# MLP second product of a decoder block: seven half products in Strassen's form for eight, on a hi/lo-split fp32 matmul

## The chip, the cores and the metric

The kernel runs on one core of one Trainium2 chip. The metric is the device time of one execution in microseconds (us), as the median of several runs. Engines: PE is TensorE (matmul), PEld its weight loads, DVE VectorE, ACT ScalarE, POOL GpSimd, SP SyncE, which here only issues DMAs.

## The reference

One inference step of a one-layer decoder, for 2048 prompt tokens and 64 sample tokens (8 sequences of 8). A mixer (forgetting attention and a matrix memory) gives `mix`; the part in question comes after it:

```python
x1  = layer_norm(ALPHA * x + mix @ w_o)          # (2112, 1024)
hid = square(relu(x1 @ w1))                      # (2112, 4096)
y   = layer_norm(ALPHA * x1 + hid @ w2)          # (2112, 1024)
```

All is fp32. The sample tokens also attend to a paged cache of 8192 past positions per sequence; that attention (the functions below it called "sample attention") is independent of the prompt tokens until its result enters `mix` of the 64 sample tokens.

## The kernel before, in words

The program is traced in phases: projections (A), prompt attention (B), output projection and first layer norm (O), MLP (C). Sample attention runs beside them in small steps: `tick(us)` adds up an amount for each piece of main work and, each time 5 us (`PACE_C`) have come together in phase C, lets one step of a generator run. A step's PE work is sQ (scores, with cached keys gathered by GpSimd into `kT`), sT (transposes) and sO (values, gathered by GpSimd into `vt`, or into `xr` while `vx["more"]` lends a second landing place). A scheduler then orders each engine's instructions once and for all by its own estimate of their times; on the chip each engine works through its list in that order and waits on semaphores.

A product in fp32 is made of three matmuls: `split_hi` (ACT, a copy into the type fp32r) and `split_lo` (DVE, the difference to it) turn an operand into hi and lo, and `mm3` (L152 to L155) adds hi·hi, hi·lo and lo·hi in PSUM. `piece` (L1058) loads 128x1024 of a weight into a `wr` buffer and splits it into `wh`, `wl`.

Phase C goes over four blocks `CB` of tokens: four tiles of 128 (W = 512), the last with the 64 sample tokens as tile 16 too (W = 576). x1 of a block lies transposed in SBUF as `x1h`, `x1l`. For each of 16 columns blocks `fc` of 256 of w1:

- `hidden(fc)`: two halves f of 128 hidden columns, each 8 x 3 matmuls into a `ph` PSUM tile (two pieces of 288 tokens where W = 576), then Relu and Square on ACT into `hq`, then its split into `hh`, `hl`.
- `output(fcs)`: two weight pieces of w2 per fc; for each token tile and each half of the 1024 columns, 2 x 3 matmuls of 128x512 into a `py` tile, and one DVE instruction (L1292, at fc 0 L1290) that adds the `py` tile to the row `y` of that token tile in SBUF.

`output` runs one fc behind `hidden`; the last two are done together, tile by tile, each tile followed at once by `layer_norm` and its store. Before that last output `load` brings in and transposes x1 of the next block (L1097). At fc 14 `vx["more"]` is taken away, at fc 13 of the third block sample attention must have ended; `sampled()` (L1215) then does the output projection and first layer norm of the 64 sample tokens, through DRAM (`dmix`, `dx1`), so that they can enter the fourth block as tile 16.

Buffers: `wr` 4, `wh` 5, `wl` 4, `hh` and `hl` 4, one `hq`, `ph` 3 and `py` 3 PSUM tiles.

```python
def mm3(ps, wh, wl, xh, xl, first, stop):
    T.matmul(ps, wh, xh, start=first, stop=False)
    T.matmul(ps, wh, xl, start=False, stop=False)
    last["PE"] = T.matmul(ps, wl, xh, start=False, stop=stop)
```

Of the kernel before, what the change touches and what calls it, by code (L numbers as in the profile page):

```python
# [52 lines left out]
def body(ctx, tc, I, O, stages):  # L53
# [95 lines left out]
        if eng is None:  # L149
            last["DVE"] = r  # L150

    def mm3(ps, wh, wl, xh, xl, first, stop):  # L152
        T.matmul(ps, wh, xh, start=first, stop=False)  # L153
        T.matmul(ps, wh, xl, start=False, stop=False)  # L154
        last["PE"] = T.matmul(ps, wl, xh, start=False, stop=stop)  # L155

    def layer_norm(x, np_, g, b, wk, tg, eng=None):
        st = wk.tile([128, 2, 6], F32, name="ln_st")
# [886 lines left out]

    def raw():

        return pcw.tile([128, 1024], F32, name="wr", bufs=4)

    def landing(n=128):  # L1050

# [12 lines left out]
    def piece(src, wr=None):  # L1064

        if wr is None:
            wr = raw().rearrange("p (k c) -> p k c", k=src.shape[1])
            SY.dma_start(wr, src)
        k = wr.shape[1]
        wh = C["pc"].tile([128, 1024], F32R, name="wh", bufs=5).rearrange("p (k c) -> p k c", k=k)  # L1070
# [31 lines left out]
    def phase_o(halves):  # L1102
# [19 lines left out]
        def weights(hf):  # L1122
            for q in range(4):
                r = halves.pop(0) if halves else half_wo(hf, q)
                if hf == 0:
                    h, l = piece(None, r)
                    if q == 0:
                        V.memset(pc.tile([128, 512], F32, name="hq", bufs=1)[:, 0:1], 0.0)
# [31 lines left out]
        unit(0, 0)  # L1160
        weights(1)
        unit(1, 0)
        gb = [bcast(I[f"ln1_{x}"], 0, D, f"{x}1", pcw, tag="wr", bufs=4) for x in "gb"]
        unit(0, 1)
        m[2] = mix(2, G)
        end(0)
# [37 lines left out]
    def phase_c():  # L1204
        es = ExitStack()
        pc, ph = C["pc"], es.enter_context(tc.tile_pool(name="ph", bufs=1, reuse_waits="tile"))
        ppc = es.enter_context(tc.tile_pool(name="ppc", bufs=1, space=PSUM, reuse_waits="tile"))
        w2, wo = I["w2"][0], I["w_o"][0]

        def vecs(l):  # L1210
            g = bcast(I[f"ln{l}_g"], 0, D, f"g{l}", pcw, tag="wr", bufs=4)
            b = bcast(I[f"ln{l}_b"], 0, D, f"b{l}", pcw, tag="wr", bufs=4)
            return g, b

        def sampled():  # L1215

            mx = pc.tile([128, 8, 64], F32, name="mxs", tag="hq", bufs=1)
            SY.dma_start(mx, dmv[:, :, S:])
            mh = ph.tile([128, 8, 64], F32R, name="mhs", tag="hh", bufs=4)
            ml = ph.tile([128, 8, 64], F32R, name="mls", tag="hl", bufs=4)  # L1220
            split_hi(mh, mx)
            split_lo(ml, mx, mh)
            y = row()
            SY.dma_start(y[:64], x_of(16))
            for c in range(4):
                ps = ppc.tile([128, 512], F32, name="py", bufs=3)[:64, :256]
# [5 lines left out]
                V.scalar_tensor_tensor(y[:64, s], y[:64, s], ALPHA, ps, op0=OP.mult, op1=OP.add)  # L1232
            layer_norm(y[:64], 64, *vecs(1), pc, "1")
            SY.dma_start(dx1[S:], y[:64])

        CB = [[0, 1, 2, 3], [4, 5, 6, 7], [8, 9, 10, 11], [12, 13, 14, 15, 16]]
        def load(ci):
            for i, t in enumerate(CB[ci]):
                x1_turn(t, i, x1_load(t), lambda: ppc.tile([128, 4, 128], F32, name="px2", tag="ph", bufs=3))
            vx["more"] = landing  # L1240

        vx["more"] = landing
        for ci, blk in enumerate(CB):
            W = sum(tok_n(t) for t in blk)
            off = {t: i * 128 for i, t in enumerate(blk)}
            xh, xl = C["x"]
            ys = {}
            pieces = [(0, 512)] if W == 512 else [(0, 288), (288, 576)]
            H = {}

            def hidden(fc):
                w1p = C.pop("w1", None) or w1_pieces(fc)
                H[fc] = []
                for f in range(2):
                    hh = ph.tile([128, 576], F32R, name="hh", bufs=4)
                    hl = ph.tile([128, 576], F32R, name="hl", bufs=4)
                    H[fc].append((hh, hl))
                    for (a, b) in pieces:
                        ps = ppc.tile([128, 512], F32, name="ph", tag="ph", bufs=3)[:, :b - a]
# [3 lines left out]
                        hq = pc.tile([128, 512], F32, name="hq", tag="hq", bufs=1)[:, :b - a]  # L1263
                        A.activation(hq, ps, AF.Relu)
                        A.activation(hq, hq, AF.Square)
                        split_hi(hh[:, a:b], hq)
                        split_lo(hl[:, a:b], hq, hh[:, a:b])
                        tick((b - a) * 0.01)

            def output(fcs):  # L1270
                w2p = [piece(w2[fc * 256 + k * 128:fc * 256 + k * 128 + 128].rearrange("(k p) c -> p k c", p=128)) for fc in fcs for k in range(2)]
                h = [x for fc in fcs for x in H.pop(fc)]
                if 15 in fcs:
                    gb = vecs(2)
                for t in blk:
                    n = tok_n(t)
                    s = slice(off[t], off[t] + n)
                    if 0 in fcs:
                        ys[t] = row()
                        with tc.issue_after(last["ACT"].ins):  # L1280
                            A.dma_start(ys[t][:n], dx1[tok_r(t):tok_r(t) + n])
                    for hf in range(2):
                        cs = slice(hf * 512, (hf + 1) * 512)
# [4 lines left out]
                        y = ys[t][:n, cs]  # L1288
                        if 0 in fcs:
                            V.scalar_tensor_tensor(y, y, ALPHA, ps, op0=OP.mult, op1=OP.add)  # L1290
                        else:
                            V.tensor_tensor(y, y, ps, op=OP.add)  # L1292
                        tick(1.28 * len(fcs))
                    if 15 in fcs:
                        layer_norm(ys[t][:n], n, *gb, pc, "2", V if ci == 3 else G)
                        d = (O["y_sample"].rearrange("b t d -> (b t) d") if t == 16 else O["y_prompt"][0, t * 128:(t + 1) * 128])
                        SY.dma_start(d, ys[t][:n])

            for fc in range(16):
                if fc == 14:  # L1300
                    vx["more"] = None
                hidden(fc)
                if fc == 15 and ci < 3:
                    take_back()
                    load(ci + 1)
                if fc > 0:
                    output([14, 15] if fc == 15 else [fc - 1])
                if fc == 13 and ci == 2:
# [394 lines left out]
def laid_in(a):  # L1703
# [10 lines left out]
    a["state_conv"] = a["state_conv"][0].reshape(NB, 3, 8, 128).transpose(3, 2, 0, 1)  # L1714
    a["state_n"] = a["state_n"][0].transpose(2, 0, 1)
    a["w_o2"] = a["w_o"][0].reshape(4, 2, 128, 2, 512).transpose(3, 0, 2, 1, 4).reshape(2, 4, 128, 1024)
    a["w1"] = a["w1"][0].reshape(2, 4, 128, 16, 256).transpose(3, 0, 2, 1, 4).reshape(16, 2, 128, 1024)
    return {k: np.ascontiguousarray(v) for k, v in a.items()}

# [11 lines left out]

# [9 lines left out]
```

## Time and profile before

| | |
|---|---|
| median of 3 runs | 3387.81 us (3377.21 to 3388.4) |
| profiled execution, its own time | 3392.21 us |
| its span, first to last instruction | 3390.5 us |
| mean granted TensorE clock | 0.985 |
| PE busy | 3263.4 us (96%) |
| DVE busy | 1884.5 us (56%) |
| ACT busy | 1361.9 us (40%) |
| POOL busy | 870.8 us (26%) |
| moved by DMA | 650.48 MB, mean 192 GB/s |

Phase C begins at about 1610 us of the span and lasts to its end. In the rows of the profile, `py` are matmuls of the second product, `ph` of the first; "128*128 128x512" are the rows and columns of the stationary operand and the shape of the result. A group row reads: line, engine, operation, output<-input, shapes, count, then busy us and mean ns of one, then idle time before it and what ended that. A row of the timeline reads: start, duration, engine, line, operation, operands, count. Matmuls overlap in the pipeline: the pace is the distance of their starts, not their duration.

### The profile page before, as it was taken

How to read it: one execution, taken by the hardware profiler on the slowest of the kernel's cores; microseconds unless marked ns; L12 is line 12 of the kernel's file. 1: busy time of each engine (PE TensorE's matmuls, PEld its weight loads, DVE VectorE, ACT ScalarE, POOL GpSimd, SP SyncE). 2: the span in 40 equal slices, each digit the busy share in tenths (PEclk: the TensorE clock that was granted, in tenths of full speed). 3: DMA queues.
4: the chain of work that ended last, by engine and by line, in shares of the span. 5: the costliest groups of instructions: out<-in, count | busy, mean ns of one | idle time of the engine just before them, and what ended most of it. 6: DMA issues, size and time to landing. Idle time of an engine off the chain costs nothing.

```text
span 3390.5 us, 58224 instructions
## 1 busy us (share of the span) xinstructions
PE 3263.4 (96%) x22065; PEld 2642.0 (78%) x22065; DVE 1884.5 (56%) x4774; ACT 1361.9 (40%) x2795; POOL 870.8 (26%) x925
## 2 busy tenths in 40 slices
PE   8999998999889999999999999999999999999998
PEld 8998998888756667676777777777776777888886
DVE  6847474464388887434444455445554445644545
ACT  4333343333278888313332333233333423433332
POOL 0131242323322222475223324323252110100000
PEclk9999999999999999999999999999999999999999
DMA  5575766766662322687777768667588444432221
GB/s 180 156 217 187 223 216 231 244 225 218 204 167 83 92 84 52 238 289 243 283 239 241 246 231 292 249 215 273 208 291 278 171 167 147 162 122 81 87 75 66
DMA packets 316001, 650.48 MB, mean 192 GB/s; under 512 B 61001, under 2 KB 175049, under 8 KB 314825
## 3 DMA queue, kind: packets, MB, share of 16 engines
q1 hardware_dynamic: 239032, 367.55, 35.4%
q0 software_dynamic: 74304, 270.57, 22.1%
q10 hardware_dynamic: 2384, 8.65, 0.7%
q8 instruction: 174, 2.85, 0.4%
q14 instruction: 107, 0.87, 0.1%
HBM read 593.82 MB, written 52.83 MB: 191 GB/s over the span
## 4 chain that ended last, share of the span: by engine, by line
PE 48%; DMA 3%; DVE 2%; issue 1%; ACT 1%; POOL 1%; another core or an unknown queue 0%; SPq 0%; POOLq 0%; ACTq 0%; DVEq 0%
PE py L153 7%; PE py L155 7%; PE py L154 7%; PE ph L153 7%; PE ph L155 7%; PE ph L154 7%; PE sO L1598 3%; PE sQ L1486 2%; DMA wr<-w 2%; PE sT L1555 1%; DVE wl L148 1%; PE pw L154 0%; PE pw L155 0%; PE pw L153 0%
## 5 line engine op out<-in xcount | busy, mean ns | idle before, releaser
L1292 DVE TENSOR_TENSOR y<-y,py 128x512 f32<-128x512 f32 (+1 forms) x476 | 324.1, 685 | 420.9 <-PE py L155 337.0
L145 ACT ACTIVATE wh<-wr 128x1024 fp32r<-128x1024 f32 x268 | 278.0, 1058 | 548.3 <-PE py L155 228.0
L153 PE MATMUL ph<-x1h,wh 128*128 128x512 f32 (+1 forms) x1280 | 458.4, 358 | 4.0 <-ACT wh L145 3.1
L154 PE MATMUL ph<-x1l,wh 128*128 128x512 f32 (+1 forms) x1280 | 456.7, 357 | 0.2 <-issue 0.2
L155 PE MATMUL ph<-x1h,wl 128*128 128x512 f32 (+1 forms) x1280 | 455.5, 357 | 0.9 <-issue 0.8
L153 PE MATMUL py<-wh,hh 128*128 128x512 f32 (+1 forms) x1088 | 438.4, 404 | 8.5 <-DVE y L1290 4.8
L1463 POOL DMA_INDIRECT kT<-cache_k,idxK x256 | 261.6, 1022 | 671.5 <-PE sQ L1486 610.3
L154 PE MATMUL py<-wl,hh 128*128 128x512 f32 (+1 forms) x1088 | 432.2, 397 | 0.6 <-DVE wl L148 0.6
L155 PE MATMUL py<-wh,hl 128*128 128x512 f32 (+1 forms) x1088 | 431.7, 397 | 0.0
L148 DVE TENSOR_TENSOR wl<-wr,wh 128x1024 fp32r<-128x1024 f32 x268 | 338.8, 1269 | 160.0 <-PE ph L155 47.1
L153 PE MATMUL pm<-xh,whi 128*128 128x256 f32 (+1 forms) x1024 | 301.9, 295 | 0.7 <-issue 0.4
L154 PE MATMUL pm<-xl,whi 128*128 128x256 f32 (+1 forms) x1024 | 297.9, 291 | 2.4 <-issue 2.3
L155 PE MATMUL pm<-xh,wlo 128*128 128x256 f32 (+1 forms) x1024 | 296.9, 290 | 2.8 <-issue 2.7
L153 PEld LDWEIGHTS ph<-x1h,wh 128*128 128x128 f32 x1280 | 241.4, 189 | 50.4 <-issue 8.9
L154 PEld LDWEIGHTS ph<-x1l,wh 128*128 128x128 f32 x1280 | 241.3, 189 | 38.9 <-issue 2.7
L155 PEld LDWEIGHTS ph<-x1h,wl 128*128 128x128 f32 x1280 | 241.2, 188 | 39.0 <-issue 2.1
L153 PEld LDWEIGHTS py<-wh,hh 128*128 128x128 f32 (+1 forms) x1088 | 202.0, 186 | 70.5 <-issue 16.3
L153 PE MATMUL pm<-whi,xh 128*128 128x256 f32 (+2 forms) x816 | 238.6, 293 | 9.9 <-ACT whi L145 8.5
L155 PEld LDWEIGHTS py<-wh,hl 128*128 128x128 f32 (+1 forms) x1088 | 202.2, 186 | 53.2 <-issue 2.5
L1574 POOL DMA_INDIRECT vt<-cache_v,idxV x158 | 159.9, 1012 | 314.8 <-PE sO L1598 240.7
L154 PEld LDWEIGHTS py<-wl,hh 128*128 128x128 f32 (+1 forms) x1088 | 202.4, 186 | 45.2 <-issue 1.6
L154 PE MATMUL pm<-wlo,xh 128*128 128x256 f32 (+2 forms) x816 | 233.9, 287 | 0.6 <-DVE wlo L148 0.6
(342 smaller groups left out, 6549.6 us busy)
## 6 DMA issues: line engine op xcount, KB each, us to landing
wr<-w SPq DMA_DIRECT2D x256, 512.0 KB
wra<-w_in SPq DMA_DIRECT2D x104, 512.0 KB
Rb<-dR SPq DMA_DIRECT2D x128, 128.0 KB
xn<-xp_t SPq DMA_DIRECT2D x16, 512.0 KB
kn<-k_prompt SPq DMA_DIRECT2D x64, 128.0 KB
qn<-dq SPq DMA_DIRECT2D x128, 64.0 KB
wr<-w_o SPq DMA_DIRECT2D x16, 512.0 KB
xr<-dmix SPq DMA_DIRECT2D x16, 512.0 KB
```

What stands on the lines that cost most here:

```text
L145: last["ACT"] = A.activation(dst, src, AF.Copy, scale=scale)
L148: r = (eng or V).tensor_tensor(dst, src, hi.bitcast(F32), op=OP.subtract)
L153: T.matmul(ps, wh, xh, start=first, stop=False)
L154: T.matmul(ps, wh, xl, start=False, stop=False)
L155: last["PE"] = T.matmul(ps, wl, xh, start=False, stop=stop)
L1292: V.tensor_tensor(y, y, ps, op=OP.add)
L1463: G.indirect_dma_start(out=piece(n), out_offset=None, in_=ck, in_offset=IO(ap=idxK[:, b, j // 2, j % 2:j % 2 + 1], axis=0))
L1486: r = T.matmul(pq[h4 * 32:h4 * 32 + 32, hg].rearrange("p (k c) -> p k c", k=2), z["qb"][:, hd], kv, start=(db == 0), stop=(db == 1), skip_ ...
L1555: T.transpose(p[:, f], z["U"][u][:, hg, f].rearrange("p k t -> p (k t)"), ident)
L1574: G.indirect_dma_start(out=vt.rearrange("p f c -> p (f c)"), out_offset=None, in_=cv, in_offset=IO(ap=idxV[:, b, (kt % 4) * 4 + kt // 4, f ...
L1598: after_ = T.matmul(po[r:r + 32], z["PT"][:, hg, 2 * f + g, pg].rearrange("p h q -> p (h q)"), vts[f][:, g, hg * 256:(hg + 1) * 256], star ...
```

## The change

`w2` is laid out on the host's side as 8 passes x 4 quarters, and phase C goes over 8 passes `p` per block. A pass takes the hidden columns of fc = p (`f1`) and fc = 8 + p (`f2`), 256 each, and the 512 tokens, in halves: a11, a21 (f1, first and second 256 tokens), a12, a22 (f2). The quarters of w2 are b11, b12 (rows of f1, first and second 512 columns), b21, b22. Seven half products, each of a 256-token operand with a quarter of w2 (2 token tiles x 2 x 3 matmuls of 128x512), take the place of eight:

| n | tokens operand | w2 operand | PSUM | added to `y` (tiles, column half) after it |
|---|---|---|---|---|
| 0 | a11 | b11 | X (starts) | 0, 1: first |
| 1 | s = a21 + a22 | b12 - b11 | Z (starts) | 2, 3: second |
| 2 | s - a11 | b22 - b12 + b11 | X | 0, 1: second |
| 3 | a12 - (s - a11) | b22 | Z | 0, 1: second |
| 4 | a11 - a21 | b22 - b12 | X | 2, 3: second |
| 5 | a12 | b21 | Y | 0, 1: first |
| 6 | a22 | b21 - (b22 - b12 + b11) | X | 2, 3: first |

X, Z and Y are pairs of `py` tiles. X is left open: DVE adds its partial sum to `y` after products 0, 2, 4 and 6 while PE goes on summing into it in between. The sums of the tokens' side are DVE instructions (128x512), those of w2 are GpSimd instructions (128x1024, in place in `wr`); operands are made two products ahead (`made`), and each is then split into hi and lo as before. Tile 16 takes part in products 0, 1, 3 and 5 with operands of its own (`hsh`, `hsl`), in matmuls of 64x512.

The order is now hidden(0, 0), hidden(0, 1), then for each p: hidden(p + 1, 0), output(p), hidden(p + 1, 1). At p = 7 the next block's `load` stands in the place of hidden, and the layer norms of all token tiles come after the last product. `vx["more"]` is taken away after output(5); sample attention must have ended, and `sampled()` follows, after pass 6 of the third block. Buffers: `wr` 5, `wh` 4, `hh` and `hl` 3 (128x512), `hq` 3 (whole, 128x2x576), `ph` 2, `py` 4. The program is built with `dynamic_dma_scratch_size=8192`, where nothing was given before.

```diff
-                        split_hi(hh[:, a:b], hq)
-                        split_lo(hl[:, a:b], hq, hh[:, a:b])
...
-            def output(fcs):
-                w2p = [piece(...) for fc in fcs for k in range(2)]
...
-                        ps = ppc.tile([128, 512], F32, name="py", bufs=3)[:n]
-                        for k in range(len(h)):
-                            wh, wl = (x[:, 0, cs] for x in w2p[k])
-                            mm3(ps, h[k][0][:, s], h[k][1][:, s], wh, wl, k == 0, k == len(h) - 1)
...
+            def output(p):
+                f1, f2 = H.pop((p, 0)), H.pop((p, 1))
+                a11, a21, a12, a22 = f1[:, :, 0:256], f1[:, :, 256:512], f2[:, :, 0:256], f2[:, :, 256:512]
+                b11, b12, b21, b22 = (raw() for _ in range(4))
+                for q, b in enumerate((b11, b12, b21, b22)):
+                    SY.dma_start(b, I["w2"][p, q])
+                s = ph.tile([128, 2, 256], F32, name="s", bufs=1)
...
+                def made(n):
+                    v = lambda o, x, y, op: V.tensor_tensor(o, x, y, op=op)
+                    g = lambda o, x, y: G.tensor_tensor(o, x, y, op=OP.subtract)
+                    w = lambda b: piece(None, b.rearrange("p (k c) -> p k c", k=2))
+                    if n == 0:
+                        v(s, a21, a22, OP.add)
+                        r = split(a11), w(b11)
+                        v(a21, a11, a21, OP.subtract)
+                        v(a11, s, a11, OP.subtract)
+                        g(b11, b12, b11)
+                        g(b12, b22, b12)
+                    elif n == 1:
+                        r = split(s), w(b11)
+                        v(s, a12, a11, OP.subtract)
+                        g(b11, b22, b11)
+                    elif n == 2:
+                        r = split(a11), w(b11)
+                        g(b11, b21, b11)
+                    else:
+                        r = (split((s, a21, a12, a22)[n - 3]), w((b22, b12, b21, b11)[n - 3]))
+                    return r
+
+                X = [ppc.tile([128, 512], F32, name="py", bufs=4) for _ in range(2)]
+                Z = None
+                ops = [made(0), made(1)]
+                plan = [("X", True, False, 0, 0), ("Z", True, False, 2, 1), ("X", False, False, 0, 1), ("Z", False, True, 0, 1),
+                        ("X", False, False, 2, 1), ("Y", True, True, 0, 0), ("X", False, True, 2, 0)]
+                extra = {0: (0, (0, 1)), 1: (0, (1,)), 3: (1, (1,)), 5: (1, (0,))}
+                for n, (kind, first_, last_, r0, half) in enumerate(plan):
+                    if n + 2 < 7:
+                        ops.append(made(n + 2))
...
+                        for k in range(2):
+                            mm3(ps, h[:, k, c], l[:, k, c], wh[:, k], wl[:, k], first_ and k == 0, last_ and k == 1, True)
+                        add(blk[r0 + i], half, ps)
+                        tick(1.28)
...
+            hidden(0, 0)
+            hidden(0, 1)
+            for p in range(8):
+                if p < 7:
+                    hidden(p + 1, 0)
+                else:
+                    if ci < 3:
+                        load(ci + 1, begun)
+                output(p)
+                if p == 5:
                     vx["more"] = None
+                if p == 6 and ci < 3:
                     take_back()
+                    begun = [x1_load(t) for t in CB[ci + 1][:2]]
+                if p < 7:
+                    hidden(p + 1, 1)
+                if p == 6 and ci == 2:
                     while acc[1] is not None:
                         tick(100.0)
                     sampled()
...
-    nc = _bacc.Bacc("TRN2", target_bir_lowering=False, num_devices=1)
+    nc = _bacc.Bacc("TRN2", target_bir_lowering=False, num_devices=1, dynamic_dma_scratch_size=8192)
```

More of the change, by code (lines that the diff above doesn't have):

```diff
@@ L150, in split_lo, with mm3 @@
             last["DVE"] = r
[L152 to L155, printed above, removed]
+    def mm3(ps, wh, wl, xh, xl, first, stop, shared=False):
+        T.matmul(ps, wh, xh, start=first, stop=False, skip_group_check=shared)
+        T.matmul(ps, wh, xl, start=False, stop=False, skip_group_check=shared)
+        last["PE"] = T.matmul(ps, wl, xh, start=False, stop=stop, skip_group_check=shared)
     def layer_norm(x, np_, g, b, wk, tg, eng=None):
@@ L1046, in raw @@
     def raw():
-        return pcw.tile([128, 1024], F32, name="wr", bufs=4)
+        return pcw.tile([128, 1024], F32, name="wr", bufs=5)
     def landing(n=128):
@@ L1294, in output, with split @@
-                    if 15 in fcs:
+                            A.dma_start(ys[t][:tok_n(t)], dx1[tok_r(t):tok_r(t) + tok_n(t)])
+                if p == 7:
+                    gb = vecs(2)
+                def split(x):
+                    h = ph.tile([128, 2, 256], F32R, name="hh", bufs=3)
+                    l = ph.tile([128, 2, 256], F32R, name="hl", bufs=3)
+                    split_hi(h, x)
+                    split_lo(l, x, h)
+                    return h, l
+                hs = []
```

111 lines of the change are left out of this document (61 added, 50 removed).

## The prediction, as it was made before the changed kernel ran

> **What bounds the kernel now.** I read the sums per engine first, then the busy time by stage, then the groups of instructions, then the waits of PE.
>
> ```profile
> span 3390.5 us, 58224 instructions
> PE 3263.4 (96%) x22065; PEld 2642.0 (78%) x22065; DVE 1884.5 (56%) x4774; ACT 1361.9 (40%) x2795; POOL 870.8 (26%) x925
> ```
>
> The stages, as columns: length, then busy us of PE, PEld, DVE, ACT, POOL with counts, granted clock, DMA share, GB/s. Phase C is the last four rows, about one block of tokens each.
>
> ```profile
> 1610.00:2060.00 450.00, 441.48 (x2705) 330.29 (x2706) 216.08 (x437) 150.24 (x244) 137.07 (x145) 1.00 0.72 248
> 2060.00:2500.00 440.00, 429.95 (x2677) 319.32 (x2676) 209.08 (x428) 145.61 (x243) 138.63 (x141) 0.99 0.71 251
> 2500.00:2930.00 430.00, 424.71 (x2382) 321.06 (x2380) 223.31 (x362) 154.42 (x229) 88.62 (x81) 1.00 0.59 201
> 2930.00:3391.00 461.00, 446.02 (x2586) 389.87 (x2584) 247.62 (x351) 158.35 (x270) 17.87 (x13) 0.99 0.28 90
> ```
>
> PE is idle for 1781 - 1742.2 = 38.8 us in all of phase C. DVE has half of its time free, ACT two thirds. So PE's instruction count sets phase C, and fewer matmuls are worth their pace, as long as what makes their operands stays hidden. Matmuls of 128x512 follow each other so:
>
> ```profile
> 1701.93 0.40 PE L155 MATMUL py<-wh,hl 128*128 128x512 f32 x1
> ...
> 1704.04 0.40 PE L155 MATMUL py<-wh,hl 128*128 128x512 f32 x1
> ```
>
> Nine steps lie between these two starts: 2.11 / 9 = 0.2344 us each, though one lasts 0.40. The longest waits of PE in phase C are small: this one has two occurrences and 4.8 us in all.
>
> ```profile
> PE py L153 <- DVE y L1290: 4.8, 2, 3.6
> ```
>
> **The change, part by part.** *Matmuls removed.* The second product had, for two fc, 2 x 2 x 4 x 2 x 3 = 96 matmuls of 128x512 per 512 tokens; a pass has 7 x 2 x 2 x 3 = 84. Tile 16 keeps its 24. So 12 x 8 passes x 4 blocks = 384 go, at 0.2344: **-90.0 us**, all on the path. The order of PE's instructions before phase C is nearly the old one, so I put nothing there.
>
> *Work added on the other engines.* The prices:
>
> ```profile
> L148 DVE TENSOR_TENSOR wl<-wr,wh 128x1024 fp32r<-128x1024 f32 x256 | 323.5, 1268 | 155.6 <-PE ph L155 43.5 <-issue 30.6 <-PE py L155 26.6
> L1292 DVE TENSOR_TENSOR y<-y,py 128x512 f32<-128x512 f32 x448 | 305.2, 686 | 403.5 <-PE py L155 319.6 <-remote 59.1 <-PE ph L155 7.6
> L148 DVE TENSOR_TENSOR hl<-hq,hh 128x512 fp32r<-128x512 f32 x92 | 63.6, 691 | 102.9 <-ACT hh L145 95.4 <-issue 4.8 <-ACT hq L1265 2.4
> L145 ACT ACTIVATE wh<-wr 128x1024 fp32r<-128x1024 f32 x255 | 264.6, 1058 | 539.4 <-PE py L155 228.0 <-PE ph L155 97.6 <-DMA wr<-w 64.6
> L145 ACT ACTIVATE hh<-hq 128x512 fp32r<-128x512 f32 x92 | 58.0, 631 | 11.7 <-remote 6.6 <-PE py L154 2.7
> L169 POOL TENSOR_TENSOR y<-y,b 128x1024 f32<-128x1024 f32 x12 | 28.8, 2402 | 31.1 <-DVE y L168 21.9 <-DVE ln_rs L164 8.7 <-issue 0.5
> ```
>
> Per pass DVE had 8 weight splits, 4 hidden splits and 16 additions, 8 x 1.268 + 4 x 0.691 + 16 x 0.686 = 23.9 us. Now it has 11, 7 and 14, and 4 sums of quarters that I price like a hidden split: 13.9 + 4.8 + 9.6 + 2.8 = 31.1. ACT gets 3 x (1.058 + 0.631) = 5.1 more. POOL gets four subtractions of 128x1024 at 2.40: 9.6. A pass is 180 x 0.2344 = 42.2 us of matmuls, with sample attention about 51 (a 440 us block less 8 x 45.0 leaves 80 for it, 10 per old pass; I take 8.5). So by sums every engine but PE has room: DVE 31 of 51, and about 4 for attention.
>
> *What DVE and POOL do to each other.* Here the sums are not enough:
>
> ```profile
> 2066.04 1.23 DVE L148 TENSOR_TENSOR wl<-wr,wh 128x1024 fp32r<-128x1024 f32 x1 [0.26 <-ACT wh L145]
> ...
> 2070.01 2.39 POOL L169 TENSOR_TENSOR y<-y,b 128x1024 f32<-128x1024 f32 x1 [3.51 <-DVE y L168]
> 2070.02 3.45 DVE L148 TENSOR_TENSOR wl<-wr,wh 128x1024 fp32r<-128x1024 f32 x1
> ```
>
> The weight split that started 0.01 us behind a POOL instruction of 2.39 ended 1.07 us after it: 3.45 in place of 1.23, so it was held for 2.2. [...] All four held in full make 31.1 + 9.6 + 4 = 44.7 us of DVE in a pass of 51: still room on average. I laid one pass of the second block's kind out by the new order of instructions. Three of the four subtractions fall under the 22.4 us of hidden matmuls and their attention steps, when DVE makes operands ahead; the fourth falls into the 84 matmuls, where DVE has 5 weight splits, 5 hidden splits, 3 of the next w1 and 13 additions, 23 us in about 24. There each operand and each freed PSUM tile comes 0.4 to 5 us before PE wants it, the tightest being the X tile's addition that PE's next write waits for. Cost on the path: between 0 (all covered) and 2.40 (one subtraction in full) per pass. I take 0.5, near the low end since the layout shows no wait, times 32: **+16**.
>
> *Third block to fourth.* Sample attention must end after pass 6 of the third block instead of fc 13, and by PE's new order the 96 small matmuls of `sampled()` stand ahead of the last output with only the x1 transposes before them; old, eight half tiles of the second product stood between. This chain was hidden:
>
> ```profile
> 2860.52 0.37 SPq L1686 DMA_DIRECT2D dmix<-mixs  x1
> ...
> 2873.15 0.64 ACT L145 ACTIVATE mhs<-mxs 128x512 fp32r<-128x512 f32 x1 [7.62 <-PE py L154]
> ...
> 2888.72 0.41 DVE L1232 SCALAR_TENSOR_TENSOR y<-y,py 64x256 f32<-64x256 f32 x1
> ...
> 2896.07 2.39 POOL L169 TENSOR_TENSOR y<-y,b 64x1024 f32<-64x1024 f32 x1 [3.87 <-DVE y L168]
> ...
> 2900.00 0.48 SPq L1234 DMA_DIRECT2D dx<-y  x1
> ```
>
> From the store of `mixs` to its reload's first use 12.6 us pass, of which I take 8 (ACT was behind other work in that row); add 5 until the store, less 3 to 4 us of transposes: PE idles 10. After `sampled()`'s last matmul come its layer norm (2888.72 to 2898.46, 9.7), a store and a reload of tile 16 of 8 again, then its transposes, which PE's order puts after only two of seven half products (5.6): 13 more, little affected by the w2 load that waits for the norm's `wr` buffer, as that runs beside it. Bounds: 12 (half) to 32 (12.6 for both round trips). **+23**. [...]
>
> *End of the program.* Old, each tile's layer norm followed its own matmuls. Now all five come after the last half product.
>
> ```profile
> 3376.40 0.40 PE L155 MATMUL py<-wh,hl 128*64 128x512 f32 x1
> ...
> 3384.93 1.22 DVE L169 TENSOR_TENSOR y<-y,b 64x1024 f32<-64x1024 f32 x1
> 3386.18 0.49 SPq L1297 DMA_DIRECT2D y_sample<-y  x1
> ```
>
> ```profile
> L160 DVE BATCH_NORM_STATS2 ln_st<-y 128x6 f32<-128x512 f32 x32 | 21.7, 687 | 0.3
> L168 DVE TENSOR_TENSOR y<-y,g 128x1024 f32<-128x1024 f32 x16 | 19.5, 1222 | 6.3 <-ACT y L167 6.3
> ```
>
> DVE ended 9.35 us after PE. One tile's norm is 2 x 0.687 + 2 x 1.222 + about 0.55 of small ones = 4.4 on DVE; five are 22, of which one statistic is done before PE ends: 21.2, **+11.8**. The last output also has no hidden matmuls to hide its operands: **+2**, bounds 0 to 6.
>
> *The other block changes.* Operands of product 1 need the last hidden columns, and four norms come at once under the next block's hidden matmuls; old, the first of these changes already had 3.6 us (the wait above). **+4** for both, bounds 0 to 12.
>
> *Sample attention's values.* With `vx["more"]` gone there is one landing place, from output(5) on: three hidden and one whole output, 19.7 us longer than three hidden and one old output, in three blocks. A gather can take long to land:
>
> ```profile
> 2017.08 12.75 DMA vt<-cache_v,idxV
> ```
>
> About 1.6 more value steps per block in that state, each waiting between 0 and that 12.75 less the 12 us between such steps, plus up to 2.40 behind a subtraction on POOL's queue; I take 1.7: 3 x 1.6 x 1.7 = **+8**, bounds 0 to 25. On POOL's queue every subtraction stands between gathers, which wait for PE; gathers for scores have three places and are further ahead.
>
> **Sum**: -90.0 + 16 + 23 + 11.8 + 2 + 4 + 8 = **-25.2 us**. The profiled execution's own time is 3392.2 (1.7 beyond its span) and would be 3367.0; it lies 4.4 above the median of the runs, so the median goes from 3387.8 to **3362.6**.
>
> **The rivals.** *All is covered (0.22).* The layout of a pass shows no wait, and the round trips through DRAM may be shorter: steady cost 0, values 0, third to fourth block 12: -90 + 12 + 11.8 + 2 + 4 = -60.2, **3327.6**. Against it: two lists in fixed order, waiting for each other, are rarely perfect.
>
> *The subtractions on POOL hold up DVE on the path (0.20), slower.* If in each pass one held split stands on PE's path, each costs 2.40: 32 x 2.40 = 76.9 in place of 16, sum +35.7, **3423.5**. By this the change turns slower than before at (16 + 25.2) / 32 = 1.3 us per pass. For it: the 3.45 us row, and DVE full during the half products. Against it: three of four subtractions have 14 us and more of cover. [...]
>
> *Value and key gathers come late (0.15), no change.* POOL's list now has 9.6 us of subtractions per pass, plus what they wait for splits, between gathers. If values add their bound of 25 and the steady cost is 0.75 per pass: -25.2 + 17 + 8 = -0.2, **3387.6**. For it: gathers of up to 12.75 us; against it: two landing places for most of the time.
>
> **How the numbers follow.** The forecast has 0.43, its own range 3345 to 3382. About 0.5% (17 us) is what a measurement of this kernel can tell from no change. Two thirds of the forecast, and all of the first rival, lie below 3370.9: 0.51 faster. A third of the forecast, most of the gathers' case and a little of POOL's: 0.29 within. The rest: 0.20 slower. The range goes from 3322, which leaves out the lower part of the first rival, to 3420, which leaves out half of the slower one.
>
> **What would show it.** Right: 384 fewer 128x512 `py` matmuls; PE's idle time in phase C up by some 60 us, with two gaps of about 10 around `sampled()`; 21 us of DVE after PE's end; DVE splits of 2 to 3.5 us wherever a POOL subtraction runs. Wrong: PE waiting in most passes for `y`, `wl` or `hl` of DVE by more than 1.3 us, sO waiting for values in most steps, or a pace of `py` matmuls other than 0.234.

## The result, and the profile after

| | before | changed |
|---|---|---|
| median | 3387.07 us (7 runs) | 3358.81 us (7 runs, 3347.64 to 3365.38) |
| ratio | | 0.9921 (95%: 0.9903 to 0.9938) |
| again on another chip | 3386.51 us | 3364.5 us, 0.9930 (0.9913 to 0.9947) |
| profiled execution, its span | 3390.5 us | 3357.1 us |

The forecast was 3362.6. By the ratio's interval the kernel is faster, by 0.6 to 1.0%. The sums per engine of the changed kernel:

```profile
span 3357.1 us, 57864 instructions
PE 3182.4 (95%) x21681; PEld 2574.7 (77%) x21681; DVE 2251.8 (67%) x5055; ACT 1505.2 (45%) x2971; POOL 1243.5 (37%) x1053
```

PE has the 384 instructions fewer, DVE 367 us more. Where the time went is seen in three windows, cut at phase C's first `ph` matmul and at PE's last matmul. Columns as in the prediction: length, then busy time per engine. First the kernel before, phase C and what follows PE's last matmul, then the changed kernel, the same two.

```profile
1609.94:3376.79 1766.85, 1742.21 (x10346) 1360.60 (x10346) 889.00 (x1564) 606.20 (x982) 381.64 (x378) 1.00 0.58 197
3376.80:3390.50 13.70, 0.00 (x0) 0.00 (x0) 7.16 (x11) 2.48 (x2) 0.60 (x2) 0.58 0.28 96
```

```profile
1608.08:3329.06 1720.98, 1665.90 (x9963) 1294.34 (x9962) 1239.58 (x1824) 745.88 (x1156) 750.53 (x502) 0.98 0.59 202
3329.10:3357.10 28.00, 0.00 (x0) 0.00 (x0) 19.65 (x33) 6.20 (x5) 6.38 (x5) 0.56 0.23 84
```

Phase C begins 1.9 us earlier. PE's busy time in it falls by 76.3 us, not by 90. Its idle time there, the length less the busy time, rises from 24.6 to 55.1 (+30.4); the 38.8 us that the prediction gave for it had the end after PE's last matmul in it. The end after PE's last matmul rises by 14.3. -1.9 - 76.3 + 30.4 + 14.3 = -33.5, which is the whole difference of the spans. Three questions follow from these four numbers: why 76.3 and not 90, where the 30.4 lie, and what makes the end longer. The waits of PE in phase C of the changed kernel (us in total, times, longest):

```profile
PE sO L1672 <- DMA vt<-cache_v,idxV: 19.7, 9, 4.4
PE px L1097 <- DMA xr<-dx: 11.7, 2, 8.2
PE px L1097 <- DVE x1l L148: 3.9, 3, 2.7
PE sO L1672 <- DMA xr<-cache_v,idxV: 3.0, 2, 2.7
PE px L1097 <- ACT hq L1258: 2.9, 1, 2.9
PE py L153 <- ACT wh L145: 2.1, 2, 1.1
PE py L153 <- ACT hh L145: 2.1, 2, 1.2
PE py L154 <- DVE wl L148: 2.0, 2, 1.5
PE py L153 <- DVE y L1268: 1.5, 3, 0.7
```

Two things stand at the top: values of sample attention (sO, 22.7 us) and x1 at the changes of block (px). The half products themselves (`py`) hardly wait: the last four rows are 7.7 us in 32 passes, and with smaller ones it is 10.1, of which 5.3 fall into the one change of block shown next.

The change from the third block to the fourth, as rows of the timeline (PE and SP's queue):

```profile
2863.42 0.43 SPq L1760 DMA_DIRECT2D dmix<-mixs  x1
2866.49 1.94 PE L1097 MATMUL px<-ident,xr 128*128 128x128 f32 x8 [3.47 <-DMA xr<-dx]
2868.31 0.37 SPq L1216 DMA_DIRECT2D mxs<-dmix  x1
2872.17 0.48 PE L153 MATMUL py<-wh,mhs 128*64 128x256 f32 x1 [1.20 <-ACT mhs L145]
...
2884.58 0.28 PE L155 MATMUL py<-wh,mls 128*64 128x256 f32 x1
...
2897.16 0.49 SPq L1232 DMA_DIRECT2D dx<-y  x1
2903.83 1.08 PE L1097 MATMUL px<-ident,xr 64*128 64x64 f32 x8 [8.23 <-DMA xr<-dx]
```

From `sampled()`'s last matmul to the store of tile 16 pass 12.6 us, and 6.7 more until its transposes start; PE's order has 24 half-product matmuls in between and then stands still for 8.23 us. All waits of PE from 2862 to 2904 add up to 18.3 us.

Idle time cost twice here. The granted clock (the column behind the five engines) around these rows of the changed kernel:

```profile
2867.00:2872.00 5.00, 3.41 (x15) 2.46 (x13) 2.44 (x4) 2.79 (x5) 0.00 (x0) 0.50 0.31 74
2872.00:2875.00 3.00, 2.83 (x13) 2.74 (x14) 2.96 (x6) 1.27 (x3) 0.00 (x0) 0.50 0.01 3
2875.00:2878.00 3.00, 3.00 (x27) 3.00 (x27) 2.96 (x5) 2.24 (x3) 0.00 (x0) 1.00 0.00 0
2904.00:2912.00 8.00, 8.00 (x30) 6.11 (x30) 7.68 (x8) 5.08 (x7) 2.39 (x1) 0.68 0.25 66
```

In 2872 to 2875 PE gets through 13 matmuls, in the next 3 us through 27 of the same kind. Half of the 6.2 busy us from 2867 to 2875, and 0.32 of the 8 us from 2904, are lost: 5.7 us beside the 18.3 of idle time. The column has 0.50 behind the wait of 3.47 us, 1.00 again in 2875 to 2878, and 0.68 in the 8 us behind the wait of 8.23. Half speed also stood behind waits for values:

```profile
2033.87 1.07 PE L1672 MATMUL sO<-vt,PTs 128*32 128x256 f32 x16 [3.01 <-DMA vt<-cache_v,idxV]
...
2407.44 1.94 PE L1672 MATMUL sO<-vt,PTs 128*32 128x256 f32 x16 [4.18 <-DMA vt<-cache_v,idxV]
...
2479.16 1.94 PE L1672 MATMUL sO<-vt,PTs 128*32 128x256 f32 x16 [2.63 <-DMA vt<-cache_v,idxV]
```

The same 16 matmuls take 1.94 us after the waits of 4.18 and 2.63 us, and 1.07 after the one of 3.01.

All stretches at half clock in phase C can be added up from the trace's record of the granted clock. Half of PE's busy time in them, which is what they cost, is 6.9 us in the kernel before and 20.0 in the changed one. That is 13.1 us more, and answers the first question, as 90.0 - 76.3 = 13.7.

### The profile page after: what moved, and what is told of

Its sections match the earlier page's. It is cut to its first block, busy times and chain, and to the rows that moved or that the text cites. A ratio compares the mean times of both kernels' runs of the same rounds, so it can differ in the third digit from the quotient of the medians.

```text
span 3357.1 us, 57864 instructions
## 1 busy us (share of the span) xinstructions
PE 3182.4 (95%) x21681; PEld 2574.7 (77%) x21681; DVE 2251.8 (67%) x5055; ACT 1505.2 (45%) x2971; POOL 1243.5 (37%) x1053
## 3 DMA queue, kind: packets, MB, share of 16 engines
q0 software_dynamic: 74304, 270.57, 22.7%
## 4 chain that ended last, share of the span: by engine, by line
PE 42%; DMA 5%; issue 2%; POOL 2%; DVE 2%; ACT 1%; POOLq 0%; ACTq 0%; DVEq 0%; SPq 0%
PE ph L153 7%; PE ph L155 7%; PE ph L154 6%; PE py L153 5%; PE py L154 5%; PE py L155 5%; DMA vt<-cache_v,idxV 3%; PE sO L1672 2%; PE sQ L1560 2%; POOL wr L1307 1%; DVE wl L148 1%; PE sT L1629 1%; POOL kT L1537 0%; DMA xr<-cache_v,idxV 0%; PE pw L154 0%
## 5 line engine op out<-in xcount | busy, mean ns | idle before, releaser
L148 DVE TENSOR_TENSOR wl<-wr,wh 128x1024 fp32r<-128x1024 f32 x364 | 479.8, 1322 | 283.4 <-ACT wh L145 281.9
L145 ACT ACTIVATE wh<-wr 128x1024 fp32r<-128x1024 f32 x364 | 382.5, 1057 | 353.7 <-PE py L155 131.9
L1307 POOL TENSOR_TENSOR wr<-wr 128x1024 f32<-128x1024 f32 x128 | 330.3, 2584 | 466.8 <-DVE wl L148 376.4
L1537 POOL DMA_INDIRECT kT<-cache_k,idxK x256 | 282.0, 1101 | 426.2 <-PE sQ L1560 363.6
L153 PE MATMUL py<-wh,hh 128*128 128x512 f32 x896 | 363.7, 407 | 6.9 <-ACT wh L145 2.1
L154 PE MATMUL py<-wl,hh 128*128 128x512 f32 x896 | 357.1, 399 | 2.0 <-DVE wl L148 2.0
L155 PE MATMUL py<-wh,hl 128*128 128x512 f32 x896 | 355.2, 398 | 0.0
L1268 DVE TENSOR_TENSOR y<-y,py 128x512 f32<-128x512 f32 x416 | 277.8, 679 | 55.8 <-PE py L155 53.4
L155 PE MATMUL pm<-whi,xl 128*128 128x256 f32 (+2 forms) x816 | 234.0, 287 | 0.0
L153 PEld LDWEIGHTS py<-wh,hh 128*128 128x128 f32 x896 | 170.3, 191 | 64.9 <-issue 12.8
```

What stands on the lines that cost most here:

```text
L145: last["ACT"] = A.activation(dst, src, AF.Copy, scale=scale)
L148: r = (eng or V).tensor_tensor(dst, src, hi.bitcast(F32), op=OP.subtract)
L153: T.matmul(ps, wh, xh, start=first, stop=False, skip_group_check=shared)
L154: T.matmul(ps, wh, xl, start=False, stop=False, skip_group_check=shared)
L155: last["PE"] = T.matmul(ps, wl, xh, start=False, stop=stop, skip_group_check=shared)
L1307: g = lambda o, x, y: G.tensor_tensor(o, x, y, op=OP.subtract)
```

## The experiments

Each run has its ratio to the kernel before on its own chip; the changed kernel stands at 0.9921 and 0.9930 by this. For each profile one row is shown: phase C from its first `ph` matmul to PE's last (length, PE busy first; the difference is PE's idle time). The changed kernel, again:

> The changed kernel itself, on the chip and in the rounds of the next three, so that they can be compared with it directly. All theories: a ratio to the kernel before of 0.990 to 0.994, as it was, so some 27 us faster.

```profile
1599.23:3326.58 1727.35, 1672.55 (x9962) 1297.91 (x9962) 1241.82 (x1824) 746.91 (x1156) 752.06 (x502) 0.98 0.59 201
```

Idle 54.8 us, as in the first profile (55.1); the busy time differs by 6.6. Two profiles of one kernel differ by some 6 us in phase C. The idle time can differ by as much: a run below that changes only the last output has 60.4 us of it, and no more waits in that output.

**Eight products in the same staging.**

```diff
-                X, Z, plan of seven, made(n)
+                ops = [split(x) for x in (a11, a12, a21, a22)]
+                for half in range(2):
+                    wts = [piece(None, b...) for b in ((b11, b21), (b12, b22))[half]]
+                    for r0 in (0, 2): ...   # a11 b + a12 b, a21 b + a22 b, summed in PSUM
```

> Seven for eight undone, all else of the staging kept: passes over f1 and f2, the same places of sample attention, the norms together at the end; the second product is the eight half products, summed over f1 and f2 in PSUM (eight additions of 128x512 per pass), with no sums of quarters on DVE or GpSimd. Buffers: hh, hl 4 and wr 4 (3 and 5 in the changed kernel). 384 matmuls of 128x512 more than the changed kernel: 90.0 us by their pace. From the run without subtractions (32 to 40 us under the changed kernel), all theories: phase C of 1688.6 + 90 = 1779 us or, as DVE's work falls too, 5 to 10 less; the time is 10 to 25 us above the kernel before, ratio 1.002 to 1.008. If the fewer matmuls were worth less than their pace, it would come out under 0.998.

```profile
1614.00:3372.24 1758.24, 1739.95 (x10347) 1360.63 (x10346) 723.62 (x1302) 603.84 (x966) 379.76 (x377) 0.99 0.59 198
3372.20:3392.80 20.60, 0.04 (x1) 0.00 (x0) 12.70 (x19) 3.72 (x3) 4.38 (x3) 0.63 0.25 89
```

3386.28 us, ratio 1.0004 (0.9990 to 1.0017): level with the kernel before, under the 1.002 expected. So the new staging as a whole brings nothing and costs nothing: against the kernel before, phase C is 8.6 us shorter, with half as many additions into `y` on DVE, and the end 6.9 longer. The whole gain of 25 to 28 us belongs to seven for eight. Against it the changed kernel (the repeat) has 67.4 us less of busy PE, 36.5 us more of idle PE (18.3 to 54.8) and 7.5 us more at the end. The half clock takes 8.3 us here and 27.0 in the repeat, so 18.7 of the 22.6 us by which 67.4 falls short of 90. The waits of sO for values are 6.8 us here.

**No subtractions on GpSimd.**

```diff
-                    g = lambda o, x, y: G.tensor_tensor(o, x, y, op=OP.subtract)
+                    g = lambda o, x, y: None
```

> The four GpSimd subtractions of w2's quarters per pass are left out (b11 is used for b12 - b11 and so on), 128 instructions of 128x1024; everything else stays. [...] Theory B, the term of the prediction (0.5 us per pass): minus 16, 3343. Theory C, the subtractions between gathers are what makes values late: minus 16 to 25 through sO's waits, 3334 to 3343, with the waits of sO for values down from 22.7 us to under 6.

```profile
1612.83:3301.43 1688.60, 1657.48 (x9963) 1290.14 (x9962) 1086.97 (x1824) 748.77 (x1156) 398.77 (x374) 0.99 0.60 206
```

3326.78 us, ratio 0.9802 (0.9783 to 0.9821): some 40 us under the changed kernel. This version leaves work out, so its `y` is not the layer's. The subtractions are far from free, though `py` hardly waits beside them (10.1 us), and the 16 us of theory B fall as a size. DVE's 1824 instructions take 1087.0 us, 153 less than in the changed kernel, where GpSimd's subtractions held them (the next two expectations call that exclusion). Idle time is 31.1 us, 24 less. One of PE's waits in phase C:

```profile
PE sO L1672 <- DMA vt<-cache_v,idxV: 7.5, 6, 4.5
```

With 2.8 us more whose end the profile doesn't show, sO waits 10.3 us, 12.4 less than with the subtractions; theory C had under 6. px waits 4.9 in place of 19.9, but at the change to the fourth block PE waits 7.4 us for `wh` instead of 8.2 for `dx`. So half of the 24 us are waits for values, and hardly any of them lay in the half products.

**The same subtractions, 16 columns wide.**

```diff
+                    g = lambda o, x, y: G.tensor_tensor(o[:, :16], x[:, :16], y[:, :16], op=OP.subtract)
```

> GpSimd's four subtractions per pass act on 16 of 1024 columns only (the rest of the quarters stays as it was): GpSimd waits for the same weight splits in the same places of its queue, with the gathers behind, but is busy for about 0.6 us in place of 2.4 and excludes DVE for as short. Without the subtractions the ratio was 0.980, against 0.992 with them. Theory A (GpSimd's waits for DVE's splits, 376 us in the trace, keep the gathers and the norms' small steps behind them): little changes, 0.989 to 0.993. Theory B (the 2.4 us themselves, as time on GpSimd's queue and as exclusion of DVE): nearly all of the gain is there, 0.979 to 0.984. In between: both.

```profile
1600.95:3303.21 1702.26, 1662.17 (x9963) 1292.22 (x9962) 1095.33 (x1824) 752.16 (x1156) 445.18 (x502) 0.99 0.59 204
```

0.9838 (0.9819 to 0.9857), again with a `y` that is not the layer's: most of the gain, with GpSimd's waits for DVE's weight splits kept (517 us, 376 in the changed kernel). It is the duration that costs: POOL is busy for 46.4 us more than without them, some 0.36 us each, where the changed kernel has 2.58. The step to no subtractions at all, 0.0036 more, is at the edge of the two intervals.

**The subtractions on DVE.**

```diff
+                    g = lambda o, x, y: v(o, x, y, OP.subtract)
```

> The four subtractions of a pass are done by DVE in place of GpSimd. They cost DVE 4 x 1.22 = 4.9 us a pass, 36 of about 51, and nothing is held any more (165 us over the medians in phase C go). Theory A (what the subtractions cost comes by way of GpSimd's queue and the exclusion): most of the 0.012 of the run without them comes back, less 5 to 8 us in the last output, where DVE has no idle time: ratio 0.981 to 0.986. Rival (the half products live from GpSimd's help: DVE's 36 us lie in the 24 us of the half products and the operands come late): PE waits for wl and hl of 1 us or more per pass, 32 us or more back: 0.990 to 1.000.

```profile
1609.63:3321.50 1711.87, 1664.11 (x9963) 1294.86 (x9962) 1232.92 (x1955) 749.42 (x1156) 407.68 (x375) 0.98 0.59 203
```

```profile
PE sO L1672 <- DMA vt<-cache_v,idxV: 15.5, 8, 3.7
PE py L153 <- ACT wh L145: 8.9, 1, 8.9
PE sO L1672 <- DMA xr<-cache_v,idxV: 6.3, 3, 2.9
```

0.9895 (0.9873 to 0.9917): between the 0.981 to 0.986 of theory A and the 0.990 of its rival, and its interval overlaps the changed kernel's. DVE's busy time does not rise (1241.8 to 1232.9): what it does itself replaces what it was held. PE's waits for operands in the half products stay small, but for one of 8.9 us at the change to the fourth block. The waits of sO stay (21.8 us), so it doesn't take subtractions on GpSimd, between the gathers, to make values late: theory C of the run without them has the right waits (they halved there) and not their reason. Done by either engine, the subtractions take some 150 us of DVE's time beside the 1087.0 of that run.

**On DVE only at the edges of a block.**

```diff
+                    g = lambda o, x, y: (V if p in (0, 7) and ci < 3 else G).tensor_tensor(o, x, y, op=OP.subtract)
```

> GpSimd's subtractions stay in passes 1 to 6, and in passes 0 and 7 of the first three blocks DVE does them: 24 of 128 move. It tells where the subtractions cost their time. Theory A (at the changes of block, where GpSimd also has the norms' small steps and additions and the next x1 waits behind them: narrow subtractions took the idle time ahead of px from 16.4 to 6.7 us): most of what DVE's subtractions brought in all passes (0.0035 of the ratio) comes with these 24: ratio 0.988 to 0.991 beside 0.993. Theory B (through late gathers in all passes): less than a third of it, 0.991 to 0.994, with px's waits unchanged.

```profile
1603.88:3314.33 1710.45, 1665.56 (x9963) 1294.04 (x9962) 1247.31 (x1848) 746.46 (x1156) 684.93 (x478) 0.99 0.59 203
```

```profile
PE py L153 <- ACT wh L145: 9.9, 1, 9.9
PE px L1097 <- DMA xr<-dx: 4.2, 2, 3.4
```

0.9882 (0.9860 to 0.9905): moving these 24 brings as much as moving all 128, as theory A has it, though the interval still touches that of the changed kernel's first measurement (0.9903 to 0.9938). px waits 6.4 us in this profile, against 16.4 and 19.9, but at the change to the fourth block a wait of 9.9 us for `wh` has come in its place. By places: in the 96 us from x1's transposes on, at the first two changes of block together, PE is idle for 7.5 us, against 15.4 and 13.8 in the changed kernel's two profiles; at the third for 18.4, against 18.6 and 16.2. In passes 1 to 6 no difference is seen between the two engines. By its length, phase C is 10.5 to 17 us shorter than the changed kernel's, and still 22 longer than without any subtraction.

**The change from the third block to the fourth.**

```diff
+                if p == 6 and ci == 2:
+                    while acc[1] is not None: tick(100.0)
+                    sampled()
                 if p < 7:
                     hidden(p + 1, 1)
-                if p == 6 and ci == 2: ...
-PACE_C = 5
+PACE_C = 4.75
```

> Sample attention runs at PACE_C 4.75 in place of 5 and ends before hidden(7, 1) of the third block; sampled() stands ahead of that hidden() and not behind it. Both round trips through DRAM (mixs to mxs, and tile 16's x1) then lie beside 96 and more matmuls. Theory A (these two chains are the cost of the change from the third block to the fourth): the waits of px for dx of 3.5 and 8.2 us, those of the short products around them (6.6 us), and the half granted clock behind them (about 5 us) go: minus 15 to 22, so 3337 to 3344. Rival: the closer pace of attention makes values later in all three blocks (sO waits up by 10 us or more) and takes half or more of it back: 3347 to 3358.

```profile
1619.22:3340.19 1720.97, 1667.28 (x9948) 1291.97 (x9946) 1239.66 (x1827) 745.50 (x1156) 754.39 (x497) 0.99 0.58 200
```

0.9906 (0.9893 to 0.9920): 5 to 8 us by the ratios and within their intervals, so inconclusive. The waits of px for `dx`, 11.7 us, fall under 1 us, but PE's idle time in phase C is 53.7 us, as it was. The rival's reason is not seen, as sO waits 19.6 us and not more; `py`, `ph` and sQ wait longer. With the subtractions on DVE, and the pace changed in phase C alone, it was tried again:

> As the run before, and sampled() stands ahead of the last hidden() of the third block, with sample attention's pace in phase C alone at 4.75 in place of 5. Theory A (the two round trips through DRAM between the third and the fourth block cost some 20 us, and their removal was eaten up by the attention steps given back to the projection phase and the first block): 8 to 18 us less than the run before. Rival (denser steps make gathers late all over): the same as the run before, within 5 us.

```profile
1609.77:3306.24 1696.47, 1662.68 (x9963) 1289.65 (x9962) 1220.99 (x1955) 746.65 (x1156) 413.10 (x375) 0.99 0.59 205
```

0.9830 (0.9810 to 0.9849), 14.8 us under the run with DVE's subtractions, and phase C is 15.4 us shorter. The waits at this place (5.3 us of px for `dx`, 8.9 for `wh`, 2.0 for `mhs`) are all but gone; sO waits 6 us less, and some 8 us of others have come. So about 15 us can be had back by moving `sampled()`; how much of it by the place and how much by the other pace of sample attention, these two runs don't tell apart.

**A longer second landing place.** `vx["more"]` is no longer taken away after output(5):

```diff
-                if p == 5:
-                    vx["more"] = None
```

> The second landing place for values is kept until take_back() after pass 6, where the changed kernel takes it away after output(5): 12 more steps of values land there. Theory A (the one landing place makes values late): the waits of sO for values, 22.7 us in phase C, lose those between pass 5 and pass 6, about a third, and with the half clock behind them 5 to 10 us go: 3349 to 3354. Theory B (a gather is late where four gathers of keys stand directly ahead of it in POOL's queue, wherever it lands): no change, 3355 to 3362, waits of sO still 18 us or more. A loss would mean that the early loads of x1 come later for it: px waits up from 23.7 us.

```profile
1612.33:3348.11 1735.78, 1676.25 (x9962) 1298.79 (x9962) 1237.72 (x1824) 747.79 (x1156) 742.26 (x502) 0.98 0.58 200
```

```profile
PE sO L1670 <- DMA vt<-cache_v,idxV: 6.0, 3, 3.4
...
PE sQ L1558 <- DMA kT<-cache_k,idxK: 4.8, 1, 4.8
PE sQ L1558 <- ACT PTs L1629: 2.8, 1, 2.8
PE sO L1670 <- DMA xr<-cache_v,idxV: 2.5, 1, 2.5
```

The waits of sO fall from 22.7 to 8.5 us, as theory A says, but the time does not: 3374.78 us, ratio 0.9942 (0.9926 to 0.9958). PE's idle time is 59.5 us; scores now wait for keys (4.8) and for ACT (2.8), and `py` waits 17.8 us in place of 9.9. Against the changed kernel's two ratios it is 4 to 7 us slower, within the intervals; so the values' waits can be moved, but the time moves with them.

**The end.** In the last output product 5 comes before product 4, and the norms of tiles 0, 1 and 16 before the last additions:

```diff
+                seq = (0, 1, 2, 3, 5, 4, 6) if p == 7 and ci == 3 else range(7)
...
+                            if n == 6 and p == 7 and ci == 3:
+                                e_.enter_context(tc.issue_after(normed[1].ins))
```

> In the last output alone, product 5 stands ahead of product 4, the layer norms of token tiles 0, 1 and 16 are given out after product 5, and the additions after product 6 wait on DVE's list for the norm of tile 1. From PE's last matmul to the end it was 28.1 us, with DVE busy for most of 24. Theory A (the end is DVE's queue of five norms): two norms of 4.4 us move under the 48 matmuls (11.2 us) of products 4 and 6, so the end falls to 18 to 20 us and the time by 8 to 10: 3349 to 3351. Rival: DVE's norms hold up the additions that PE's last product waits for, so PE ends later by as much: 3355 to 3362.

Windows of this run, 20 us ahead of PE's last matmul and what follows it (DVE's busy time is the third):

```profile
3322.00:3342.00 20.00, 19.26 (x83) 14.42 (x81) 19.84 (x32) 5.16 (x8) 0.55 (x1) 1.00 0.01 2
3342.00:3369.10 27.10, 0.02 (x1) 0.00 (x0) 19.10 (x32) 6.20 (x5) 5.83 (x4) 0.59 0.24 87
```

3363.21 us, 0.9914 (0.9899 to 0.9930): no change; the end is 27.1 us in place of 28.0. Nor does PE wait longer in the last output, as the rival had it. Neither theory had what the rows suggest: DVE is busy for 19.84 of the last 20 us (19.27 of 20.1 in the changed kernel), so a norm that is given out earlier only changes places in a queue that is full. Nor did taking the last output's subtractions off DVE help, on top of the run with 0.9830:

> The run of ratio 0.983 (DVE's subtractions, early sampled()), with GpSimd's subtractions in the very last output only, where DVE has no idle time. Theory A (DVE's list sets the end there): 4.9 us of DVE go to GpSimd, 3 to 5 us less, ratio 0.981 to 0.982. Rival (held splits give it back): 0.983 to 0.985.

0.9857 (0.9832 to 0.9882), not the 0.981 to 0.982 expected; the end is 27.5 us beside 27.3.

**The differences of w2 made once.** They are the same for all four blocks:

```diff
+                    if ci:      # blocks 1 to 3: loaded from dB
+                        r = split(...), piece(src[n]...)
...
+                    keep = lambda b, j: A.dma_start(dB[p][j], b)      # block 0
```

> The four differences of w2's quarters are made once, in the first block (by DVE), stored to DRAM, and loaded in the other three blocks, so that 96 of the 128 subtractions go, on any engine; 12.6 MB more are written and 37.7 MB more read. sampled() stands ahead of the third block's last hidden(), pace 4.75 in phase C, as in the run of ratio 0.983. Theory A (the subtractions cost by engine time, and 29 GB/s more beside 200 to 260 are free): another 10 to 20 us under that run, ratio 0.977 to 0.980. Rival (gathers become later with the added traffic: their waits up from 15.7 us): 0.981 to 0.988.

```profile
1599.40:3287.66 1688.26, 1658.01 (x9963) 1286.86 (x9962) 1123.02 (x1856) 748.73 (x1156) 401.63 (x374) 0.99 0.68 238
```

3318.99 us, ratio 0.9816 (0.9792 to 0.9841): 66 us under the kernel before by the medians, and the fastest version here that computes all of it, though its ratio is not clear of 0.9830. DVE is 98 us less busy than in the run of 0.9830, and the DMA share rises from 0.59 to 0.68. The trace has 16.8 MB more written, not 12.6, and the 37.7 more read. sO waits 16.6 us, beside 15.6, so the rival's later gathers are not seen; nor are the 10 to 20 us of theory A.

## Why the prediction was right, point by point

The total came out within 4 us (-28.3 for -25.2 by the medians), by terms that were off in both directions. The mechanism (fewer matmuls at their pace, less what the added work costs at the few places without cover) was right; that the sum came so near is in part luck.

- **384 matmuls at their pace, -90.** PE's busy time fell by 76.3, or by 67.4 between the repeat and the eight products. The matmuls went as counted; the rest is, but for 1 to 4 us, the halved clock behind longer idle times (13.1 and 18.7 us), which the sum had at nothing. The trace of before shows it too: the gap of 3.63 us that the prediction had in its list of waits (as 3.6) was followed by half speed:

```profile
2096.60:2100.00 3.40, 3.40 (x8) 2.73 (x9) 2.42 (x11) 0.00 (x0) 0.00 (x0) 0.50 1.03 410
```

- **Held splits in the steady passes, +16.** DVE is held, but the cost does not come by the path that the term gave, and it is larger. In these groups of DVE (busy us, mean ns) of phase C

```profile
L148 DVE TENSOR_TENSOR wl<-wr,wh 128x1024 fp32r<-128x1024 f32 x356 | 468.5, 1319 | 283.4 <-ACT wh L145 281.9 <-issue 0.4 <-PE ph L155 0.2
L148 DVE TENSOR_TENSOR hl<-hq,hh 128x512 fp32r<-128x512 f32 x160 | 147.6, 923 | 5.1 <-ACT hh L145 5.1
L148 DVE TENSOR_TENSOR hl<-s,hh 128x512 fp32r<-128x512 f32 x64 | 75.2, 1175 | 0.3 <-ACT hh L145 0.3
L1306 DVE TENSOR_TENSOR s<-hq 128x512 f32<-128x512 f32 x64 | 68.6, 1072 | 34.1 <-ACT hq L1259 33.4
L1306 DVE TENSOR_TENSOR hq<-hq 128x512 f32<-128x512 f32 x32 | 44.0, 1377 | 0.6
L1306 DVE TENSOR_TENSOR hq<-s,hq 128x512 f32<-128x512 f32 x32 | 33.6, 1050 | 0.3
```

the means lie above 1.22 and 0.691 us: by count, 35 + 37 + 31 + 24 + 22 + 11 = 160 us of holding, of the 307 that 128 subtractions held in full would make. The run without subtractions bears this out: with the same 1824 instructions DVE is busy for 153 us less there. This is what the prediction's row of 3.45 us in place of 1.23 had shown once. Yet `py` waits no longer than before (10.1 us in all, 9.6 before). The rival that put 2.40 us per pass on the path is refuted, and PE's waits for operands, by which the forecast came to 0.5 per pass, are not seen. But the subtractions do cost some 40 us in all, more than the 16: 10 to 17 of it at the changes of block, where moving 24 of them to DVE brings that much; the rest goes only when they go or become short. The idle PE time is 31.1 us without them, 40.1 at some 0.36 us each, 47.8 on DVE, whose busy time has 146 us more by them, and 55.1 on GpSimd at 2.58, each in one profile. Of the 24 us of idle time that go without them, 12 are waits of sO for values, and most of the others lie at the changes of block; by what chain subtractions on either engine make values late, the runs don't show.
- **Third block to fourth, +23.** 18.3 us of idle time and 5.7 of half clock, against 1.5 of idle time there before: +22.5. The size was right; the shape was not (gaps of 10 and 13 were expected, where the numbers given for the second make 9.7 + 8 - 5.6 = 12; 3.5 and 8.2 came, with 6.6 us of short waits, most of them for operands, and the half clock).
- **The end, +11.8.** 14.3. DVE ended 24.1 us after PE and not 21.2. Its work there was 19.7 us, less than counted; the rest is gaps within the norms, in which it waits for ACT (2.4) and for GpSimd's small step (1.8), and these the sum had left out. The eight products, with 7 us less for DVE to do there, end 20.6 us after PE, so half of the added 14.3 is the norms' new place and half is DVE's work for seven products.
- **Last output without cover, +2, and other block changes, +4.** PE waited 0.9 us in the last output. At the first two changes of block it waited 2.65 and 2.95 us and three times 1.2 to 1.3, so 9.5 against 3.6 before: +5.9. Both are near enough.
- **Values, +8.** 22.7 us against 0.7: near the bound of 25, and the added term that was furthest off. (Its 19.7 us are right for two hidden and one old output, by the code; the sentence says three.) The reason given (one landing place, and subtractions between gathers) holds only in part: with the place kept, sO waits 8.5 us, but nothing is gained; without subtractions it waits 10.3, but with DVE's in place of GpSimd's still 21.8. Scores had waited 9.6 us before (4.9 of it for nothing that the profile shows) and wait no more, a gain that the sum did not have. What makes values late stays open.

So 90 came out as 76, six added terms of 65 came out as 45 (30.4 in phase C and 14.3 at the end), and the two errors cancel in the main. By the count of the prediction's own sign, idle time with the end in it, PE has 44.7 us more and not some 60. The rival in which gathers come late had its mechanism nearly in full, but without the added steady cost that it needed to reach no change.

## What to carry to other kernels

Taking matmuls from an engine that is 96% busy pays only as far as everything else keeps its distance: here 90 us of matmuls became 28, because the added work and the new order lengthened the chains at the few places where nothing covers them, made values late, and because 8 of the 9 idle times of 2.6 us and more in phase C also had half clock behind them. Price the changes of stage and the end first; in the steady loop, with DVE busy for 72% of phase C, PE hardly waited for the half products' operands. Moving the two round trips under other work, with the subtractions on DVE, made some 52 us out of the change's 28. Making what is the same in every block once (here the differences of the weights) made it 66, but the last step is within the intervals.

## What was not expected of the hardware

The clock halved behind a wait of 2.63 us (sO at 2479.16, 1.94 us for 16 matmuls) and did not behind one of 3.01 (2033.87, 1.07 us). So the length of a wait alone did not tell whether half clock came behind it; what did, the runs don't show. Mostly it came: in the profiles of the two kernels, 9 of the 10 waits of PE in phase C of 2.6 us and more had half clock behind them. And DVE's total busy time was the same whether it did 128 subtractions itself (1232.9 us in phase C) or was held by GpSimd's (1241.8); without any it was 1087.0.
